# One layer of a hybrid conformer on one core: search vectors in PSUM, a second load buffer, eight gate matrices ahead of attention, and stores issued by ScalarE

## The chip, the cores and the metric

The kernel runs on one core of a Trainium2 chip. The metric is the device time of one execution in microseconds (us). Engines are called PE (TensorE, matmuls), PEld (its weight loads), DVE (VectorE), ACT (ScalarE), POOL (GpSimd) and SP (SyncE, which here only starts DMAs); SPq, DVEq and ACTq are their sequencers.

## The reference

One layer of a streaming encoder, in float32, on 1024 prompt frames and 64 sample frames (1088 together) of width 1024:

```python
h = x + 0.5 * _swiglu(x, ffn1_norm, ffn1_w_in, ffn1_w_out)
u = _rms(h, mix_norm)
z = u @ w_in                       # q | k | v | q_idx | k_idx | w_idx | conv_in | gate
...
score = jnp.einsum('bqh,bqhs->bqs', wi, jax.nn.relu(s))     # s: indexer queries x indexer keys
_, sel = lax.top_k(score, top)                              # top = min(256, L // 4)
...                                # softmax attention of each query over its selected keys
conv_out = jax.nn.silu(_layernorm(dc, conv_ln_g, conv_ln_b)) @ conv_w_out   # dc: depthwise conv, 31 taps
g_a, g_c = jnp.split(jax.nn.sigmoid(gate + b_gate), 2, axis=-1)
merged = g_a * (attn @ attn_w_out) + g_c * conv_out
h = h + merged @ w_out
h = h + 0.5 * _swiglu(h, ffn2_norm, ffn2_w_in, ffn2_w_out)
```

and a final norm. Outputs are the frames and the new keys, values, indexer keys and conv states.

## The kernel before

**Arithmetic.** Every float32 product is made of three matmuls: each operand is split into a high and a low part, and `mm3` adds hi x hi, hi x lo and lo x hi (L154, L155, L156). Weights come raw from HBM by SP (`raw`, L135), ACT rounds them to the high part (`whi`, L136), POOL subtracts to get the low part (`wlo`, L137). Activations are split the same way by `split`: the high part on ACT (L170), the low part on DVE or POOL (L171). A matmul of 128 x 128 weights moves one chunk of frames; there are three chunks, of 364, 362 and 362 frames.

**Stages.** The first feed-forward part; the projections, the conv (each tap a product `pd` on ACT, L694, and an addition on POOL, L695) and the indexer scores `Y` (L807 to L815), one row for each frame in seven tiles; then the search; then attention; then the second feed-forward part and the norm.

**The search** finds, for every frame, the threshold that leaves the wanted number of scores. It runs on DVE alone (L854 to L912). A first threshold comes from mean and spread of each row (L854 to L867). Six rounds follow, each with seven counts (L871, one per tile, result in `cnt`), and after each but the last some ten operations on 128x7 vectors (L876 to L888) that move the threshold `thr`. Then each tile gets the scores below the threshold (`F`, L897), their eight largest (L898), as many of them marked as the count is short (L899, L900), and a mask (`bias`, L904, with its count `seen`). Flags are formed and a branch (L914) is taken on DVE; its body is a slower search for rows whose count is off. The search has a high scheduling priority.

**K, V and the first queries.** `load_k` (L712 to L717), the load of V and `load_q` (L700 to L708) each bring raw data into a buffer `raw2` and split it. K, V and q share that buffer.

**Gates.** `gates` makes 16 matrices of gates, each in three chunks of 24 matmuls: 48 chunks. Each chunk's PSUM bank goes through a tanh on ACT (`sg`, L942), and SP stores it (L943). The first `GPRE` matrices are written ahead of attention, the others are background work inside it.

**Attention.** 36 units: nine tiles of queries by four pairs of heads. `soft` makes logits (`lg`, L989 and L990), adds the mask and takes the maximum on DVE (L992, `mb`), exponentials on ACT (L1002), scaling; `turn` transposes the weights into `pt` and splits them (`ph`, `pl`); `values` multiplies with V into `pv`, ACT copies that to `oh` (L1042), and SP stores it (L1043). Logits are made two units ahead. Between the steps `fill` takes `FILL[tile]` steps from a background generator: the rest of the gates, norm and output product of the conv (`gc`, L1122 to L1124), the merge of the third chunk (`ga`, L1147 to L1154), its product with `w_out` (`hr`, L1165, with loads at L1172 and stores at L1173) and the merge of the second chunk. Once attention is over, `h` is loaded again in three pieces (L1242) and the other products with `w_out` follow.

**Order.** A scheduler places the instructions of each engine by priorities and by its own model of time, so that the order on an engine isn't that of the code. Each engine works its list in order. SP's DMAs and, where it starts any, ACT's are counted on eight shared semaphores, and a DMA that takes one over waits for the one before it.

Of the kernel before, what the change touches and what calls it, by code (L numbers as in the profile page):

```python
# [95 lines left out]
def search_table():  # L96

    nd = NormalDist()
    t = np.zeros((P, 14, NT), np.float32)
    for n, (t0, rows, k0, L, top_) in enumerate(STILES):  # L100
        for half in range(2):
            r = slice(64 * half, 64 * half + 64)
            A = L - 64 * (1 - half) * (rows == P)
            z = nd.inv_cdf(1 - (top_ - 4) / A)
            t[r, 0, n], t[r, 1, n] = z, 1 / (A * nd.pdf(z))
        t[:, 2:6, n] = top_ - 3.9, top_, 1 / L, NEG * (L - top_)
    t[:, 6:] = np.tile(np.arange(8), NT).reshape(8, NT)
    return t.reshape(P, -1)


class Kern:
# [342 lines left out]
    def run(self):  # L454
        tc, nc, a = self.tc, self.nc, self.a
        PS = bass.MemoryType.PSUM
        with ExitStack() as top:
# [240 lines left out]
            def load_q(pool, src, t0, rows, qpool=None, qb=2, n=1280):  # L698

                raw = pool.tile([P, n], F32, name="raw2", tag="raw2")[:, 0:1024]  # L700
                raw = raw.rearrange("p (h c) -> p h c", h=8)[:, :, :rows]
                for i in range(4):
                    nc.sync.dma_start(raw[32 * i:32 * i + 32],
                                      src[i % 2, :, t0:t0 + rows].rearrange("(h r) c -> r h c", r=32))
                qt = (qpool or pool).tile([P, 8, P], F32R, name="qt", tag="qt", bufs=qb)[:, :, :rows]
                nc.scalar.activation(qt, raw, AF.Copy)
                nc.vector.tensor_tensor(qt[64:], raw[64:], qt[64:], op=ALU.subtract)
                return qt  # L708

            def load_k(pool, r0, name, tmp=None):  # L710
                kh = pool.tile([P, KCOLS], F32R, name=f"kh{name}")
                kl = pool.tile([P, KCOLS], F32R, name=f"kl{name}")  # L712
                raw = (tmp or pool).tile([P, 1280], F32, name="raw2", tag="raw2")[:, 0:KCOLS]
                for i in range(4):
# [46 lines left out]
            for i in (0, 1):  # L761
# [5 lines left out]
            small = lambda n, w=NT: kp.tile([P, w], F32, name=n)  # L767
            cnt, seen, exc, was, step, slope, gate, thr, unit = (
                small(n) for n in ("cnt", "seen", "exc", "was", "step", "slope", "gate", "thr", "unit"))
            sums = small("sums", 2 * NT)  # L770
            best = kp.tile([P, NT, 8], F32, name="best")
            rank = kp.tile([P, NT, 8], F32, name="rank")
            flags = kp.tile([P, 32], F32, name="flags")
# [22 lines left out]
            for n in SORD:  # L796
# [56 lines left out]
            v = nc.vector  # L853
            v.tensor_tensor(step, sums[:, 0:2 * NT:2], sums[:, 1:2 * NT:2], op=ALU.add)  # L854
# [4 lines left out]
            v.tensor_scalar(exc.bitcast(I32), slope.bitcast(I32), -0.5, 1597463007.0, op0=ALU.mult, op1=ALU.add)  # L859
            for i in range(2):  # L860
                v.tensor_tensor(gate, slope, exc, op=ALU.mult)
                v.scalar_tensor_tensor(gate, gate, -0.5, exc, op0=ALU.mult, op1=ALU.mult)
                v.scalar_tensor_tensor(exc, gate, 1.5, exc, op0=ALU.add, op1=ALU.mult)
            v.tensor_tensor(slope, slope, exc, op=ALU.mult)
            v.tensor_tensor(thr, slope, quant, op=ALU.mult)
            v.tensor_tensor(thr, thr, step, op=ALU.add)
            v.tensor_tensor(unit, slope, inv, op=ALU.mult)  # L867
            for r in range(ROUNDS):
                for n in range(NT):
                    rows, y0, L = rows_of(n)  # L870
                    v.tensor_scalar(spare(n), Y[:rows, y0:y0 + L], thr[:rows, n:n + 1], 0.0,  # L871
                                    op0=ALU.is_ge, op1=ALU.add, accum_out=cnt[:rows, n:n + 1])
                if r == ROUNDS - 1:
                    break
                exc, was = was, exc
                v.tensor_tensor(exc, cnt, goal, op=ALU.subtract)  # L876
                v.tensor_tensor(gate, exc, exc, op=ALU.mult)
                if r:
                    v.scalar_tensor_tensor(slope, was, 0.001, exc, op0=ALU.add, op1=ALU.subtract)
                    v.reciprocal(slope, slope)  # L880
# [3 lines left out]
                else:  # L884
                    v.tensor_copy(step, exc)
                v.scalar_tensor_tensor(gate, gate, 16.9, step, op0=ALU.is_gt, op1=ALU.mult)
                v.tensor_tensor(gate, gate, unit, op=ALU.mult)
                v.tensor_tensor(thr, thr, gate, op=ALU.add)  # L888

            v.tensor_tensor(gate, wanted, cnt, op=ALU.subtract)  # L890
            v.tensor_tensor(rank, gate.rearrange("p (n o) -> p n o", o=1).to_broadcast([P, NT, 8]),
                            zt[:, 6 * NT:].rearrange("p (n o) -> p n o", o=8), op=ALU.is_gt)
            v.tensor_scalar(rank, rank, 2 * STOP, -STOP, op0=ALU.mult, op1=ALU.add)
            for n in range(NT):
                rows, y0, L = rows_of(n)
                f = F[:rows, y0:y0 + L]
                v.scalar_tensor_tensor(f, spare(n), -STOP, Y[:rows, y0:y0 + L], op0=ALU.mult, op1=ALU.add)  # L897
                v.max(best[:rows, n, :], f)  # L898
                v.tensor_tensor(best[:rows, n, :], best[:rows, n, :], rank[:rows, n, :], op=ALU.min)  # L899
# [36 lines left out]
            def gates(ms, pool):  # L936
                for m, off in ms:
                    wt = self.wload(off, 1024)
                    for c, (c0, w) in enumerate(CHUNKS):
                        p = uproj(wt, c)  # L940
                        sg = pool.tile([P, WMAX], F32, name="sg", tag="sg", bufs=3)[:, :w]
                        nc.scalar.activation(sg, p, AF.Tanh, bias=hb[:, m:m + 1], scale=0.5)  # L942
                        nc.sync.dma_start(d_g[m, :, c0:c0 + w], sg)  # L943
                        yield
# [83 lines left out]
            def values(u, slot, ph, pl):  # L1028
# [9 lines left out]
                if last:  # L1038
                    if u.h0 == 6:
                        done.add(u.i)  # L1040
                    oh = ap_.tile([64, 256], F32, name="oh", tag="oh", bufs=2)[:, :n]
                    nc.scalar.activation(oh, u.pv, AF.Copy)  # L1042
                    nc.sync.dma_start(  # L1043
                        d_at[64 * u.h0:64 * u.h0 + 128, u.t0:u.t0 + u.rows].rearrange("(h d) c -> d h c", d=64),
# [196 lines left out]
            for c0, w in CHUNKS[::-1]:  # L1241
                nc.sync.dma_start(h[:, :, c0:c0 + w], d_h[:, :, c0:c0 + w])  # L1242
            tp = self.pool(top, "tp2", 6)
# [182 lines left out]
```

## Time and profile before

| | us |
|---|---|
| median of 3 runs (lowest, highest) | 2435.06 (2434.07, 2438.32) |
| the profiled execution | 2435.61 |
| its span | 2433.8 |
| PE busy | 2307.9 (95%) |
| DVE busy | 1677.8 (69%) |
| POOL busy | 1404.1 (58%) |
| ACT busy | 1146.8 (47%) |

The span is what the profile shows between the first and the last instruction; 1.8 us lie around it. The profiled execution is 0.55 us above the median. A row of the timeline or of the groups names the line, the engine, the operation, the tile written and the tiles read. A row of waits reads "engine tile line <- who released it: total us, times, longest".

### The profile page before, as it was taken

Reading aid. Unit: us, or ns where it says so; the run is one execution under the profiler, and the core shown is the slowest. Engines: PE = TensorE matmul, PEld = TensorE weight load, DVE = VectorE, ACT = ScalarE, POOL = GpSimd, SP = SyncE. Lnnn points to the kernel's source line nnn. Section 1 sums busy time; section 2 is a strip of 40 time slices with the busy share of each in tenths; the row PEclk is TensorE's granted clock in tenths of the full one; section 3 lists DMA queues with packets and bytes.
Section 4 is the critical chain, followed back from the end, with each engine's and each line's share of the span. In section 5 each row is a group of like instructions: output and inputs, shape, how many; then the busy total and the mean of one; then the engine's idle time right before and its main releaser. Section 6 shows DMA issues by size and latency. Waiting matters only on the chain.

```text
span 2433.8 us, 43946 instructions
## 1 busy us (share of the span) xinstructions
PE 2307.9 (95%) x16762; PEld 2278.1 (94%) x16762; DVE 1677.8 (69%) x3600; ACT 1146.8 (47%) x2189; POOL 1404.1 (58%) x861
## 2 busy tenths in 40 slices
PE   5999999999999999989699888799999999999998
PEld 5999999999999999989699888799999999999997
DVE  7666678666678386689634897358666677776676
ACT  5434445434346556865554664235443445433343
POOL 4555555555557786888662444457555555555554
PEclk9999999999999999999899999899999999999999
DMA  4222223223224344333223345752232322332223
GB/s 164 96 96 96 93 99 122 98 88 105 96 90 137 126 136 126 95 113 100 63 83 110 102 143 173 261 175 101 87 105 87 100 99 80 110 104 102 96 96 116
DMA packets 130118, 271.92 MB, mean 112 GB/s; under 512 B 18032, under 2 KB 77296, under 8 KB 129904
## 3 DMA queue, kind: packets, MB, share of 16 engines
q1 hardware_dynamic: 129904, 269.08, 33.1%
q8 instruction: 132, 2.16, 0.4%
q14 instruction: 82, 0.67, 0.1%
HBM read 230.34 MB, written 38.75 MB: 111 GB/s over the span
## 4 chain that ended last, share of the span: by engine, by line
PE 40%; DVE 6%; DMA 3%; issue 1%; ACT 1%; POOL 0%; SPq 0%; DVEq 0%; ACTq 0%
PE ps L154 12%; PE ps L156 12%; PE ps L155 12%; DMA ga<-d_g 1%; PE pt L1016 1%; DVE ga L1153 1%; DMA d_mp<-gc 1%; PE lg L989 1%; PE lg L990 0%; PE ps L184 0%; DVE pr L992 0%; PE pv L154 0%; DMA hr<-d_h 0%; DMA gc<-d_g 0%; PE pv L155 0%
## 5 line engine op out<-in xcount | busy, mean ns | idle before, releaser
L137 POOL TENSOR_TENSOR wlo<-raw,whi 128x1024 fp32r<-128x1024 f32 (+1 forms) x187 | 435.4, 2333 | 421.9 <-ACT whi L136 406.7
L154 PE MATMUL ps<-x,wp 128*128 128x272 f32 x1760 | 508.8, 291 | 11.2 <-DVE spare L302 9.2
L156 PE MATMUL ps<-x,wp 128*128 128x272 f32 x1760 | 506.3, 291 | 1.0 <-DVE wp L171 0.4
L155 PE MATMUL ps<-x,wp 128*128 128x272 f32 x1760 | 506.9, 289 | 0.0
L154 PE MATMUL ps<-x,whi 128*128 128x272 f32 (+2 forms) x1544 | 483.2, 313 | 18.2 <-ACT sg L942 8.8
L156 PE MATMUL ps<-x,wlo 128*128 128x272 f32 (+2 forms) x1544 | 481.5, 312 | 0.0
L155 PE MATMUL ps<-x,whi 128*128 128x272 f32 (+2 forms) x1334 | 412.3, 309 | 0.0
L154 PE MATMUL ps<-gh,whi 128*128 128x272 f32 x1408 | 400.0, 289 | 6.8 <-DVE spare L302 5.0
L155 PE MATMUL ps<-gl,whi 128*128 128x272 f32 x1408 | 404.9, 289 | 0.0
L156 PE MATMUL ps<-gh,wlo 128*128 128x272 f32 x1408 | 403.8, 288 | 0.0
L171 POOL TENSOR_TENSOR wlo<-raw,whi 128x1024 fp32r<-128x1024 f32 x88 | 220.1, 2502 | 263.8 <-ACT whi L170 260.6
L154 PEld LDWEIGHTS ps<-x,wp 128*128 128x128 f32 x1760 | 333.1, 189 | 12.2 <-ACT wp L170 12.2
L155 PEld LDWEIGHTS ps<-x,wp 128*128 128x128 f32 x1760 | 333.6, 190 | 0.0
L156 PEld LDWEIGHTS ps<-x,wp 128*128 128x128 f32 x1760 | 331.0, 189 | 2.3 <-DVE wp L171 1.7
L154 PEld LDWEIGHTS ps<-x,whi 128*128 128x128 f32 x1544 | 293.1, 190 | 20.3 <-ACT sg L942 9.3
L171 POOL TENSOR_TENSOR wp<-s,wp 128x512 fp32r<-128x512 f32 x176 | 258.7, 1470 | 90.0 <-ACT wp L170 90.0
L136 ACT ACTIVATE whi<-raw 128x1024 fp32r<-128x1024 f32 (+1 forms) x187 | 190.7, 1020 | 234.8 <-PE ps L155 127.2
L156 PEld LDWEIGHTS ps<-x,wlo 128*128 128x128 f32 x1544 | 292.9, 190 | 1.0
L442 DVE SCALAR_TENSOR_TENSOR h<-ps,h 128x272 f32<-128x272 f32 x384 | 164.7, 439 | 184.7 <-PE ps L156 184.2
L695 POOL TENSOR_TENSOR ac<-ac,pd 128x559 f32<-128x559 f32 x180 | 259.8, 1444 | 45.8 <-ACT pd L694 15.5
L154 PEld LDWEIGHTS ps<-gh,whi 128*128 128x128 f32 x1408 | 263.0, 189 | 8.3 <-DVE spare L302 5.7
L156 PEld LDWEIGHTS ps<-gh,wlo 128*128 128x128 f32 x1408 | 265.8, 189 | 0.0
(236 smaller groups left out, 4815.3 us busy)
## 6 DMA issues: line engine op xcount, KB each, us to landing
raw<-wf SPq DMA_DIRECT2D x334, 512.0 KB, 3.2
raw<-wf SPq DMA_DIRECT2D x32, 384.0 KB, 3.0
d_g<-sg SPq DMA_DIRECT2D x32, 181.0 KB, 1.9
d_h<-h SPq DMA_DIRECT2D x2, 2176.0 KB, 10.4
y<-t SPq DMA_DIRECT2D x32, 136.0 KB, 1.8
raw<-d_q SPq DMA_DIRECT2D x32, 128.0 KB, 2.7
raw<-d_qi SPq DMA_DIRECT2D x24, 128.0 KB, 3.0
d_g<-sg SPq DMA_DIRECT2D x16, 182.0 KB, 2.0
```

What stands on the lines that cost most here:

```text
L136: nc.scalar.activation(hi[:, :n], raw[:, :n], AF.Copy)
L137: self.weng.tensor_tensor(lo[:, :n], raw[:, :n], hi[:, :n], op=ALU.subtract)
L154: t.matmul(out, wh, xh, start=first, stop=False)
L155: t.matmul(out, wh, xl, start=False, stop=False)
L156: t.matmul(out, wl, xh, start=False, stop=last)
L171: (eng or nc.vector).tensor_tensor(lo, x, hi, op=ALU.subtract)
L442: nc.vector.scalar_tensor_tensor(x, p, 0.5, x, op0=ALU.mult, op1=ALU.add)
L695: nc.gpsimd.tensor_tensor(ac, ac, pd, op=ALU.add)
L989: nc.tensor.matmul(o, q, kh[:, ks:ks + pw], start=True, stop=False)
L1016: nc.tensor.transpose(pt[:kn, o:o + r], u.pr[hh][:, kk:kk + kn], ident[:r, :r])
L1153: nc.vector.scalar_tensor_tensor(ga, mpt, 0.5, ga, op0=ALU.mult, op1=ALU.add)
```

## The change

It has four parts.

1. `GPRE` goes from 2 to 8, so eight gate matrices (24 chunks) stand ahead of attention instead of two (6 chunks), and `FILL` for the sample tile from 4 to 2.
2. Search: the vectors `goal`, `over`, `slope`, `gate` and `cen` and the table `rank` lie in one PSUM bank, `srch`, instead of SBUF. Where two SBUF vectors were the operands of a 128x7 operation, one of them is now in PSUM; for that the excess is formed twice (`exc` in SBUF, `over` in PSUM), and the mean as well (`mean`, `cen`). Both inputs remain in SBUF for the first sum and for a few others, among them the mask. The rank test is against `goal` with a shifted table, which decides alike.
3. `raw2` has two buffers in attention's pools, and one in the indexer's.
4. ACT, not SP, starts the 48 gate stores, the 36 stores of attention outputs and the three reloads of `h`.

```diff
-GPRE = 2
+GPRE = 8
...
-FILL = {7: 1, 6: 1, 8: 4, 5: 1, 4: 1, 3: 2, 2: 2, 1: 2, 0: 2}
+FILL = {7: 1, 6: 1, 8: 2, 5: 1, 4: 1, 3: 2, 2: 2, 1: 2, 0: 2}
...
-    t[:, 6:] = np.tile(np.arange(8), NT).reshape(8, NT)
+    t[:, 6:] = np.tile(np.arange(8) - 3.4, NT).reshape(8, NT)
...
-                raw = pool.tile([P, n], F32, name="raw2", tag="raw2")[:, 0:1024]
+                raw = pool.tile([P, n], F32, name="raw2", tag="raw2", bufs=2 if n == 1280 else 1)[:, 0:1024]
...
-                raw = (tmp or pool).tile([P, 1280], F32, name="raw2", tag="raw2")[:, 0:KCOLS]
+                raw = (tmp or pool).tile([P, 1280], F32, name="raw2", tag="raw2", bufs=1 if tmp else 2)[:, 0:KCOLS]
...
-            quant, inv, goal, wanted, per, expect = (zt[:, i * NT:(i + 1) * NT] for i in range(6))
+            quant, inv, target, wanted, per, expect = (zt[:, i * NT:(i + 1) * NT] for i in range(6))
...
-                nc.scalar.activation(spare(n), y, AF.Square, accum_out=cnt[:rows, n:n + 1])
+                nc.scalar.activation(spare(n), y, AF.Square, scale=L ** -0.5, accum_out=cnt[:rows, n:n + 1])
...
-            v.tensor_tensor(step, sums[:, 0:2 * NT:2], sums[:, 1:2 * NT:2], op=ALU.add)
-            v.tensor_tensor(step, step, per, op=ALU.mult)
-            v.tensor_tensor(cnt, cnt, per, op=ALU.mult)
-            v.tensor_tensor(slope, step, step, op=ALU.mult)
+            bank = lgi.tile([P, 512], F32, name="srch", tag="lgi")
+            goal, over, slope, gate, cen = (bank[:, 16 * i:16 * i + NT] for i in range(5))
+            rank = bank[:, 128:128 + 8 * NT].rearrange("p (n o) -> p n o", o=8)
+            v.tensor_copy(goal, target)
+            v.tensor_tensor(gate, sums[:, 0:2 * NT:2], sums[:, 1:2 * NT:2], op=ALU.add)
+            v.tensor_tensor(cen, gate, per, op=ALU.mult)
+            v.tensor_tensor(mean, gate, per, op=ALU.mult)
+            v.tensor_tensor(slope, cen, mean, op=ALU.mult)
...
+                v.tensor_tensor(over, cnt, goal, op=ALU.subtract)
                 v.tensor_tensor(exc, cnt, goal, op=ALU.subtract)
-                v.tensor_tensor(gate, exc, exc, op=ALU.mult)
+                v.tensor_tensor(gate, exc, over, op=ALU.mult)
                 if r:
-                    v.scalar_tensor_tensor(slope, was, 0.001, exc, op0=ALU.add, op1=ALU.subtract)
+                    v.scalar_tensor_tensor(slope, was, 0.001, over, op0=ALU.add, op1=ALU.subtract)
                     v.reciprocal(slope, slope)
...
-                    v.tensor_copy(step, exc)
+                    v.tensor_scalar(step, over, 1.0, None, op0=ALU.mult)
...
-            v.tensor_tensor(gate, wanted, cnt, op=ALU.subtract)
+            for n in range(NT):
+                rows, y0, L = rows_of(n)
+                f = F[:rows, y0:y0 + L]
+                count(n, spare(n))
+                v.scalar_tensor_tensor(f, spare(n), -STOP, Y[:rows, y0:y0 + L], op0=ALU.mult, op1=ALU.add)
+                v.max(best[:rows, n, :], f)
+            v.tensor_tensor(gate, goal, cnt, op=ALU.subtract)
...
-            raw = ak.tile([P, 1280], F32, name="raw2", tag="raw2").rearrange("p (b d) -> p b d", d=P)
+            raw = ak.tile([P, 1280], F32, name="raw2", tag="raw2", bufs=2).rearrange("p (b d) -> p b d", d=P)
...
-                        nc.sync.dma_start(d_g[m, :, c0:c0 + w], sg)
+                        nc.scalar.dma_start(d_g[m, :, c0:c0 + w], sg)
...
-                    nc.sync.dma_start(
+                    nc.scalar.dma_start(
                         d_at[64 * u.h0:64 * u.h0 + 128, u.t0:u.t0 + u.rows].rearrange("(h d) c -> d h c", d=64),
...
-                nc.sync.dma_start(h[:, :, c0:c0 + w], d_h[:, :, c0:c0 + w])
+                nc.scalar.dma_start(h[:, :, c0:c0 + w], d_h[:, :, c0:c0 + w])
```

In the changed kernel the lines from the search on have numbers that are higher by three to ten: the gate store is L953, the attention store L1053, the logits L999 and L1000, the reload L1252, the branch L924.

The scheduler gives the engines new orders. Three places matter.

SP around the two K loads (`raw2<-d_k`), before:

```order
L135 DMA raw_14249<-wf 128x1024
L715 DMA raw2_13612<-d_k_60 32x1216 x4
L943 DMA d_g_64<-sg_13675 128x364
L943 DMA d_g_64<-sg_13703 128x362
L943 DMA d_g_64<-sg_13731 128x362
L715 DMA raw2_13621<-d_k_60 32x1216 x4
L135 DMA raw_14388<-wf 128x1024
```

and now:

```order
L135 DMA raw_14100<-wf 128x1024
L715 DMA raw2_13618<-d_k_60 32x1216 x4
L715 DMA raw2_13627<-d_k_60 32x1216 x4
L937 DMA raw2_13635<-d_v_61 128x1152
L938 DMA raw2_13635<-d_v_61 64x128
L703 DMA raw2_13642<-d_q_58 32x8x64 x3
L135 DMA raw_14190<-wf 128x1024
```

Three gate stores stood between the two K loads; now the second follows the first at once, and V and the first queries come right behind.

ACT at the same place, now (the K splits are `kh0` and `kh1`):

```order
L952 ACTIVATE sg_13709<-ps_13684,hb_81 128x362
L170 ACTIVATE kh0_13616<-raw2_13618 128x1216
L953 DMA d_g_64<-sg_13709 128x362
L694 ACTIVATE pd_12241<-ci_12162,par_77 128x559
L170 ACTIVATE kh1_13625<-raw2_13627 128x1216
L694 ACTIVATE pd_12244<-ci_12162,par_77 128x559
```

The gate store (L953) now stands in ACT's own list, one or two places behind the tanh that it stores.

PE at the first logits that need the search's end, before:

```order
L154 MATMUL ps_14484<-x_9442,whi_14479 128x364
L155 MATMUL ps_14484<-u_9450,whi_14479 128x364
L156 MATMUL ps_14484<-x_9442,wlo_14480 128x364
L989 MATMUL lg_13872<-kh0_13610,qt_13641 64x192 [waits DVE_49]
L990 MATMUL lg_13872<-kl0_13611,qt_13641 64x192
L989 MATMUL lg_13897<-kh1_13619,qt_13641 64x192 [waits DVE_49]
```

and now:

```order
L1000 MATMUL lg_14413<-kl0_13617,qt_13647 64x192
L154 MATMUL ps_14453<-x_9436,whi_14448 128x364 [waits DVE_49]
L155 MATMUL ps_14453<-x_9444,whi_14448 128x364
L156 MATMUL ps_14453<-x_9436,wlo_14449 128x364 [waits Pool_49]
...
L155 MATMUL ps_14481<-x_9445,whi_14448 128x362
L999 MATMUL lg_14418<-kh0_13616,qt_13647 64x192 [waits DVE_49]
L1000 MATMUL lg_14418<-kl0_13617,qt_13647 64x192
L999 MATMUL lg_14443<-kh1_13625,qt_13647 64x192 [waits DVE_49]
```

The fourth logits matmul of attention (`lg_13872`, now `lg_14418`) waits for DVE's first mask addition after the branch. Between the first gate matmul and it PE's list holds 529 gate matmuls before and 609 now, counted down the list; after the first 580 of these stands `ps_14453`, whose bank is that of the search's vectors, so that it waits for the search to end. Later in PE's list, the gates are through when 72 logits matmuls are (92 before), the merge of the third chunk begins after 182 of them (after all 208 before), and the merge of the second chunk stands among the last units of attention, where before it came after them.

More of the change, by code (lines that the diff above doesn't have):

```diff
@@ L767, in run @@
             small = lambda n, w=NT: kp.tile([P, w], F32, name=n)
-            cnt, seen, exc, was, step, slope, gate, thr, unit = (
-                small(n) for n in ("cnt", "seen", "exc", "was", "step", "slope", "gate", "thr", "unit"))
+            cnt, seen, exc, was, step, mean, thr, unit, root = (
+                small(n) for n in ("cnt", "seen", "exc", "was", "step", "mean", "thr", "unit", "root"))
             sums = small("sums", 2 * NT)
             best = kp.tile([P, NT, 8], F32, name="best")
-            rank = kp.tile([P, NT, 8], F32, name="rank")
             flags = kp.tile([P, 32], F32, name="flags")
@@ L858, in run @@
+            v.tensor_copy(goal, target)
[3 more added lines that the diff above has]
+            v.tensor_tensor(slope, cen, mean, op=ALU.mult)
             v.tensor_tensor(slope, cnt, slope, op=ALU.subtract)
-            v.tensor_scalar(exc.bitcast(I32), slope.bitcast(I32), -0.5, 1597463007.0, op0=ALU.mult, op1=ALU.add)
+            v.tensor_scalar(root.bitcast(I32), slope.bitcast(I32), -0.5, 1597463007.0, op0=ALU.mult, op1=ALU.add)
@@ L860, in run @@
             for i in range(2):
[L861 to L864, printed above, removed]
+                v.tensor_tensor(gate, slope, root, op=ALU.mult)
+                v.scalar_tensor_tensor(gate, gate, -0.5, root, op0=ALU.mult, op1=ALU.mult)
+                v.scalar_tensor_tensor(root, gate, 1.5, root, op0=ALU.add, op1=ALU.mult)
@@ L865, in run, with count @@
+            v.tensor_tensor(slope, slope, root, op=ALU.mult)
             v.tensor_tensor(thr, slope, quant, op=ALU.mult)
-            v.tensor_tensor(thr, thr, step, op=ALU.add)
+            v.tensor_tensor(thr, thr, cen, op=ALU.add)
             v.tensor_tensor(unit, slope, inv, op=ALU.mult)
-            for r in range(ROUNDS):
-                for n in range(NT):
[L870 to L874, printed above, removed]
+            def count(n, out):
+                rows, y0, L = rows_of(n)
+                v.tensor_scalar(out, Y[:rows, y0:y0 + L], thr[:rows, n:n + 1], 0.0,
+                                op0=ALU.is_ge, op1=ALU.add, accum_out=cnt[:rows, n:n + 1])
@@ L875, in run @@
+            for r in range(ROUNDS - 1):
+                for n in range(NT):
+                    count(n, spare(n))
                 exc, was = was, exc
+                v.tensor_tensor(over, cnt, goal, op=ALU.subtract)
                 v.tensor_tensor(exc, cnt, goal, op=ALU.subtract)
-                v.tensor_tensor(gate, exc, exc, op=ALU.mult)
+                v.tensor_tensor(gate, exc, over, op=ALU.mult)
                 if r:
-                    v.scalar_tensor_tensor(slope, was, 0.001, exc, op0=ALU.add, op1=ALU.subtract)
+                    v.scalar_tensor_tensor(slope, was, 0.001, over, op0=ALU.add, op1=ALU.subtract)
@@ L888, in run @@
                 v.tensor_tensor(thr, thr, gate, op=ALU.add)
-            v.tensor_tensor(gate, wanted, cnt, op=ALU.subtract)
+            for n in range(NT):
+                rows, y0, L = rows_of(n)
+                f = F[:rows, y0:y0 + L]
+                count(n, spare(n))
+                v.scalar_tensor_tensor(f, spare(n), -STOP, Y[:rows, y0:y0 + L], op0=ALU.mult, op1=ALU.add)
+                v.max(best[:rows, n, :], f)
+            v.tensor_tensor(gate, goal, cnt, op=ALU.subtract)
             v.tensor_tensor(rank, gate.rearrange("p (n o) -> p n o", o=1).to_broadcast([P, NT, 8]),
@@ L896, in run @@
                 f = F[:rows, y0:y0 + L]
-                v.scalar_tensor_tensor(f, spare(n), -STOP, Y[:rows, y0:y0 + L], op0=ALU.mult, op1=ALU.add)
-                v.max(best[:rows, n, :], f)
                 v.tensor_tensor(best[:rows, n, :], best[:rows, n, :], rank[:rows, n, :], op=ALU.min)
```

## The prediction

> **What bounds the kernel now.** I read the page's busy rows first, then the waits of the whole run, then the windows and the timeline around the longest of them.
>
> ```profile
> span 2433.8 us, 43946 instructions
> PE 2307.9 (95%) x16762; PEld 2278.1 (94%) x16762; DVE 1677.8 (69%) x3600; ACT 1146.8 (47%) x2189; POOL 1404.1 (58%) x861
> ```
>
> TensorE (PE) is busy for 2307.9 of 2433.8 us, and the change takes no matmul away. So it can only give back PE's idle time, about 126 us, or a stretch at a lower clock. The waits say where that idle time lies near the changed lines:
>
> ```profile
> PE lg L989 <- DVE mb L992: 24.3, 5, 20.4
> PE ps L154 <- ACT sg L942: 8.8, 1, 8.8
> PE ps L154 <- DVE ga L1152: 14.6, 6, 6.7
> PE ps L154 <- DVE hr L1165: 5.1, 1, 5.1
> ACT kh L170 <- DMA raw<-d_k: 7.2, 1, 7.2
> ```
>
> (Columns: total us, times, longest.) The first row is one wait of 20.4 us for the threshold search on VectorE (DVE), the second one wait of 8.8 us for a gate activation. On the timeline both have their place:
>
> ```profile
> 1087.58 0.67 PE L154 MATMUL ps<-x,whi 128*128 128x364 f32 x1 [8.83 <-ACT sg L942]
> 1088.05 0.51 PE L155 MATMUL ps<-x,whi 128*128 128x364 f32 x1
> 1091.08 0.51 PE L156 MATMUL ps<-x,wlo 128*128 128x364 f32 x1
> 1152.93 0.33 PE L155 MATMUL ps<-u,whi 128*128 128x364 f32 x1
> 1153.10 0.33 PE L156 MATMUL ps<-x,wlo 128*128 128x364 f32 x1
> 1173.81 0.42 PE L989 MATMUL lg<-kh,qt 128*64 128x192 f32 x1 [20.38 <-DVE mb L992]
> ```
>
> Gate matmuls start 0.167 us apart (1152.93, 1153.10). PE stops at about 1153.4 with its gate work in front of the logits used up, and goes on at 1173.81. The windows show what follows, in four stretches up to the second feed-forward part (columns: length, busy of PE, PEld, DVE, ACT, POOL, granted clock, DMA share, GB/s):
>
> ```profile
> 1173.80:1328.00 154.20, 153.51 (x991) 148.40 (x992) 70.19 (x176) 85.94 (x167) 90.25 (x50) 0.99 0.26 84
> 1328.00:1488.00 160.00, 144.39 (x987) 134.27 (x985) 138.24 (x364) 98.57 (x222) 75.22 (x45) 0.97 0.45 137
> 1488.00:1585.00 97.00, 76.58 (x410) 74.27 (x411) 44.24 (x67) 29.72 (x50) 41.45 (x20) 0.88 0.71 239
> 1585.00:1677.00 92.00, 86.68 (x530) 85.19 (x529) 64.26 (x134) 41.92 (x82) 58.70 (x35) 1.00 0.42 137
> ```
>
> PE is idle there for 0.7, 15.6, 20.4 and 5.3 us: 42 us that the change may shrink or grow.
>
> **The change, part by part.** *The search.* DVE runs it without a gap:
>
> ```profile
> 1057.27 0.89 DVE L854 TENSOR_TENSOR step<-sums 128x7 f32<-128x7 f32 x1
> 1061.24 1.25 DVE L861 TENSOR_TENSOR gate<-slope,exc 128x7 f32<-128x7 f32 x1
> 1064.01 0.17 DVE L861 TENSOR_TENSOR gate<-slope,exc 128x7 f32<-128x7 f32 x1
> 1127.84 2.32 DVE L888 TENSOR_TENSOR thr<-thr,gate 128x7 f32<-128x7 f32 x1
> 1166.24 0.19 DVE L912 TENSOR_REDUCE flag<-turned 128x1 int32<-128x32 f32 x1
> 1173.40 0.35 DVE L992 CUSTOM_DVE_ANT_0 pr<-lg,bias 64x192 f32<-64x192 f32 x1 [6.98 <-DVEq L914]
> ```
>
> From 1057.27 to 1166.43 it takes 109.2 us, and the branch at L914 another 7.0. One and the same instruction, L861, takes 1.25 us and then 0.17. Of the 128x7 rows 22 are long, the first and the last of them being 1057.27 and 1127.84; together they take 28.5 us. All but a copy have two inputs in SBUF, and all lie while POOL is adding. Two neighbouring rows of equal size show what one PSUM operand does to that:
>
> ```profile
> L327 DVE TENSOR_TENSOR s<-ps,raw 128x512 f32<-128x512 f32 x88 | 60.0, 682 | 0.0
> L332 DVE TENSOR_TENSOR s<-raw,s 128x512 f32<-128x512 f32 x88 | 101.6, 1155 | 0.0
> L207 DVE TENSOR_TENSOR rt<-rv,ps 128x3 f32<-128x3 f32 (+1 forms) x9 | 1.4, 154 | 0.2
> ```
>
> With `ps` in PSUM 682 ns, with both in SBUF 1155. L207 shows that a tiny operation with a PSUM input costs 154 ns, no more than the 0.17 of the SBUF ones. The change puts one operand of 21 of the 22 long operations into PSUM (the sum of `sums` stays): 27.6 - 21 x 0.17 = 24.1 us less. Bounds: 0, if the long rows have another cause, and 24.1. I take 24.1, since the pair L327 and L332 is the nearest row. About six operations are added: 6 x 0.2 = 1.2.
>
> The Trainium skill, "Perfetto Trace Analysis", section "Optimizing Scalar/DVE Operations", speaks against it: it gives DVE an access overhead of about 60 ns on SBUF and 125 ns on PSUM. By that some 70 small operations would lose 65 ns each, an estimate of 4.6 us, and the search would gain 18 instead of 23. The 154 ns of L207 does not bear it out, so I leave it out.
>
> A shorter search has a price of its own:
>
> ```profile
> L897 DVE SCALAR_TENSOR_TENSOR F<-bias,Y 128x384 f32<-128x384 bf16 (+6 forms) x7 | 13.1, 1929 | 0.0
> L904 DVE SCALAR_TENSOR_TENSOR bias<-F,fill 128x384 bf16<-128x384 f32 (+6 forms) x7 | 5.3, 801 | 0.0
> 1150.99 2.85 POOL L695 TENSOR_TENSOR ac<-ac,pd 128x559 f32<-128x559 f32 x2 [3.56 <-ACT ac L690]
> ```
>
> L904 (the mask) now runs from 1159 on, after POOL's last tap at 1153.8; L897, with the same shapes and POOL busy, takes 1929 ns. Begun 17 us earlier, the seven masks meet POOL: between 0 and 7 x 1.1 = 7.9 us; I take 7. The search ends at 1057.3 + 109.2 - 24.1 + 1.2 + 7 = 1150.6, the branch at 1157.6, and the first `mb` is there at 1158.0, instead of 1173.7.
>
> *The K loads.* What made PE wait 8.8 us is on SP's queue:
>
> ```profile
> 1060.78 9.01 SPq L943 DMA_DIRECT2D d_g<-sg  x3
> 1081.20 0.35 SPq L943 DMA_DIRECT2D d_g<-sg  x1
> 1477.32 0.58 SPq L1043 DMA_DIRECT2D d_at<-oh  x1
> 1524.72 0.58 SPq L1242 DMA_DIRECT2D h<-d_h  x1
> SPq L943 <- ACT sg L942: 106.8, 34, 6.7
> ```
>
> The three gate stores stand on SP between the first and the second K load and hold it until 1074.08; the second K split on ScalarE (ACT) then waits 7.2 us for that load, and the gate activation queued behind it frees no PSUM bank for PE. With a second `raw2` buffer and the stores on ACT, the two loads stand next to each other, so the 8.8 us go. Behind that wait 13 matmuls start some 0.30 us apart instead of 0.167 (the second and the last of them are at 1088.05 and 1091.08): about 1.8 us more. Together 10.6; below, if K still comes late, 0.
>
> *More gates ahead (GPRE, FILL).* In PE's order 609 gate matmuls, not 529, stand between the last indexer work and the fourth logits matmul, the one that waits for `mb`: 80 x 0.167 = 13.3 us of work pulled forward. The first 51 of them lead to a PSUM bank that the search holds to its end.
>
> *Sum at PE.* PE reaches that bank at 1153.4 - 10.6 + 51 x 0.167 = 1151.3, and the search ended at 1150.6: no wait. After 29 more matmuls, 1156.1, it waits until 1158.0: 1.9 us are left of 20.4. Gain: 8.8 + 1.8 + 20.4 - 1.9 = 29 us. Without a shorter search PE would stand at the bank from 1151.3 to 1167.4, and later for another 2.8: gain 12. So this term lies between 12 (or about 2, with K late too) and 31.
>
> *What follows.* Gates end earlier against attention, and the merges of the third and second chunk, which ran with attention over (idle 20.4 us), are now interleaved with its end: I take 8 of the 19.7 us of the `ga` and `hr` rows (14.6 + 5.1) as hidden, bounds 0 and 19.7. Against that: attention's DVE, at 138.2 of 160 us, gets part of the merges' work too, and I charge 3 (bounds 0 and 15.6, as much again as that window is idle now). The 48 gate stores, 36 attention stores and 3 reloads now cost ACT 48 x 0.35 + 36 x 0.58 + 3 x 0.58 = 39 us of issue. ACT's load is 98.6 of 160 in the densest window; 36 x 0.58 = 21 us more make it 120 of 160, so most lies beside other work. But many stores share a semaphore with a load of SP's and must wait for its landing, and behind a waiting store stand the next exponentials and splits: I charge 4, bounds 0 and 36. The reload of h, 4.35 MB at the end of merging, where DMA moves 239 GB/s already, gets 3, bounds 0 and 10 (its landing takes 7 to 10 us). Tail: -8 + 3 + 4 + 3 = +2.
>
> 2435.6 - 29 + 2 = 2408.6 for the profiled execution, which lies 0.55 above the median: **2408 us**.
>
> The Trainium skill, "DMA: Bandwidth & Descriptors", section "Issuing engines are not separate DMA queues", holds that issuing from several engines saves only the sequencer's time to start a transfer. By that rule moving the stores is worth nothing where SP is off the path, and the 10.6 us would rest on the second buffer alone. No row of this trace separates the two.
>
> **Rivals.** *The search does not get shorter* (PSUM operands don't help, or DVE waits instead for the K, V and q splits that now stand in its first two rounds). For it: the row below has two SBUF inputs as well and is never long, so I don't know the whole rule. Against it: L327 and L332. It gives 12 - 2 = 10 us: 2425.
>
> ```profile
> L886 DVE SCALAR_TENSOR_TENSOR gate<-gate,step 128x7 f32<-128x7 f32 x5 | 0.8, 167 | 0.2
> ```
>
> *The tail takes the idle time back.* Gates that are done cannot fill PE any more while softmax runs. For it: the first window after the search is full (153.5 of 154.2) just because gates fill it, and 13.3 us of them are gone from there. Against it: 112 background steps still meet 112 fill slots. It gives 2408 + 13 = 2421.
>
> *Slower: ACT's own stores stop ACT.* ACT works in order. Each of the 36 attention stores comes right behind its copy of `oh`, ahead of the next exponentials; if issue (0.58) and a wait of some 0.4 for a load's landing (whose median is 3.2 us for a weight) fall on the chain each time, that is 36 us: 2408 + 36 = 2444. It decides from 27 us, 0.75 per store. For it: SP waited 106.8 us in total in those places, so the stores do have something to wait for; these are waits for ACT itself, which fall away when ACT issues. Against it: ACT has 61 us free in that window.
>
> ```profile
> raw<-wf SPq DMA_DIRECT2D x334, 512.0 KB, 3.2
> h<-d_h SPq DMA_DIRECT2D x2, 1448.0 KB, 7.1
> ```
>
> **How the numbers follow.** My forecast, 2408 (its own range 2397 to 2418), has 0.62; the search not shorter, 2425, 0.12; the tail takes it back, 2421, 0.12; slower, 2444, 0.14. About 0.2%, 4.9 us, is what a measurement of this kernel can tell from no change. The first and third case are faster but for a small part; of the second a quarter, and of the fourth a third, fall within 0.2%: faster 0.82, same 0.08, slower 0.10. The range goes from 2390, where the merges' idle time and the masks' price both fall away, to 2435, which leaves out most of the last case.
>
> **What would show it.** Right: the 128x7 rows of the search at 0.15 to 0.25 us and the search near 93 us; no PE wait for `sg` near 1080; the wait for `mb` under 5 us; the four windows' PE idle together near 42. Wrong: long small rows in the search still there, PE waits with ACT as releaser after 1160, or ACT waiting on a DMA in front of its stores. A sum of idle time in the tail over 70 us would turn the sign.

## The result, and the profile after

| | before | after |
|---|---|---|
| median | 2435.23 us (2434.07 to 2438.32) | 2395.25 us (2394.14 to 2395.94) |
| ratio, 95% interval | | 0.9833 (0.9816 to 0.985) |
| span of the profiled execution | 2433.8 us | 2392.3 us |

The change makes the kernel 40 us faster, 1.5 times the 27 us that were forecast. The time lies inside the whole range of the prediction (2390 to 2435), but 2 us below 2397 to 2418, the range of its main case. The page of the changed kernel, its span and busy rows:

```profile
span 2392.3 us, 43870 instructions
PE 2300.3 (96%) x16762; PEld 2272.8 (95%) x16762; DVE 1658.8 (69%) x3606; ACT 1146.8 (48%) x2189; POOL 1407.1 (59%) x861
```

PE's 16762 matmuls are the same, but PE is busy for 7.6 us less, and idle for 33.9 us less. Windows tell where. Three of the kernel before (columns as in the prediction: length, PE, PEld, DVE, ACT, POOL, clock, DMA share, GB/s):

```profile
0.00:1055.00 1055.00, 1016.75 (x7468) 1008.74 (x7469) 722.42 (x1524) 520.80 (x982) 646.77 (x427) 0.99 0.32 108
1055.00:1700.00 645.00, 573.76 (x3626) 554.06 (x3626) 444.73 (x993) 323.62 (x626) 362.13 (x208) 0.95 0.42 133
1700.00:2433.80 733.80, 717.36 (x5672) 715.34 (x5670) 510.67 (x1086) 302.40 (x582) 395.22 (x227) 0.99 0.29 98
```

and of the changed kernel, whose last one is cut to the same length:

```profile
0.00:1055.00 1055.00, 1016.41 (x7467) 1008.14 (x7468) 725.91 (x1524) 520.27 (x982) 646.15 (x427) 0.99 0.33 108
1055.00:1658.50 603.50, 566.63 (x3630) 549.58 (x3629) 423.31 (x998) 324.74 (x626) 367.49 (x208) 0.97 0.45 142
1658.50:2392.30 733.80, 717.27 (x5670) 715.09 (x5668) 509.57 (x1085) 301.82 (x582) 393.48 (x227) 0.99 0.30 98
```

First and last part agree to 0.4 us, so all of the 41.5 us lie in the middle, 645.0 against 603.5. There PE's idle time falls from 71.2 to 36.9 and its busy time, for the same matmuls but for a few at the edges, from 573.8 to 566.6. The waits of PE after, in that part:

```profile
PE lg L999 <- ACT sg L952: 6.9, 1, 6.9
PE pv L154 <- ACT oh L1052: 6.7, 4, 3.5
PE lg L999 <- DVE mb L1002: 2.6, 4, 1.7
PE ps L154 <- DVE ga L1162: 7.8, 5, 3.8
PE ps L154 <- DVE hr L1175: 0.6, 1, 0.6
```

The waits of 8.8 and 20.4 us are gone; a new one of 6.9 us stands at the first logits. So the sum of the prediction can be redone with what was measured:

| us, change against before | forecast | measured |
|---|---|---|
| idle at K loads and search (29.2 before) | -27.3 | -22.3 |
| PE busy, less time at a low clock | -1.8 | -7.1 |
| idle in the rest up to the second feed-forward part (42 before) | +2 | -12.0 |
| sum | -27 | -41.5 |

The search is what the prediction said it would be. Two of DVE's groups before (busy us, mean ns):

```profile
L888 DVE TENSOR_TENSOR thr<-thr,gate 128x7 f32<-128x7 f32 x5 | 4.1, 815 | 0.2
L881 DVE TENSOR_TENSOR slope<-slope,step 128x7 f32<-128x7 f32 x4 | 3.8, 942 | 0.1
```

and its groups after:

```profile
L894 DVE TENSOR_TENSOR thr<-thr,srch 128x7 f32<-128x7 f32 x5 | 0.8, 163 | 0.2
L887 DVE TENSOR_TENSOR srch<-srch,step 128x7 f32<-128x7 f32 x4 | 0.7, 174 | 0.1
L914 DVE SCALAR_TENSOR_TENSOR bias<-F,fill 128x384 bf16<-128x384 f32 (+6 forms) x7 | 11.4, 1672 | 0.0
L919 DVE TENSOR_TENSOR srch<-seen,zt 128x7 f32<-128x7 f32 x1 | 1.2, 1234 | 0.0
```

and its timeline:

```profile
1057.50 0.90 DVE L857 TENSOR_TENSOR srch<-sums 128x7 f32<-128x7 f32 x1
1151.44 0.18 DVE L922 TENSOR_REDUCE flag<-turned 128x1 int32<-128x32 f32 x1
1159.75 0.35 DVE L1002 CUSTOM_DVE_ANT_0 pr<-lg,bias 64x192 f32<-64x192 f32 x1 [8.13 <-DMA d_g<-sg]
```

What was L888 (815 ns) is now 163 ns, what was L881 (942) is 174. The masks went from 801 to 1672 ns: they do meet POOL, and cost 6.1 us. From 1057.5 to 1151.6 the search takes 94.1 us.

### The profile page after: what moved, and what is told of

Its sections match the earlier page's. It is cut to its first block, busy times and chain, and to the rows that moved or that the text cites. A ratio compares the mean times of both kernels' runs of the same rounds, so it can differ in the third digit from the quotient of the medians.

```text
span 2392.3 us, 43870 instructions
## 1 busy us (share of the span) xinstructions
PE 2300.3 (96%) x16762; PEld 2272.8 (95%) x16762; DVE 1658.8 (69%) x3606; ACT 1146.8 (48%) x2189; POOL 1407.1 (59%) x861
## 4 chain that ended last, share of the span: by engine, by line
PE 76%; DVE 9%; DMA 6%; POOL 4%; issue 2%; ACT 2%; SPq 0%; ACTq 0%; DVEq 0%; POOLq 0%
PE ps L154 24%; PE ps L156 24%; PE ps L155 24%; POOL ac L695 3%; DMA ga<-d_g 1%; PE pt L1026 1%; PE lgi L806 1%; PE lgi L807 1%; DMA d_h<-hr 1%; DVE ga L1163 1%; DMA raw<-wf 1%; DMA raw<-d_k 1%; PE ps L184 1%; DMA d_mp<-gc 1%; DVE t L229 1%
## 5 line engine op out<-in xcount | busy, mean ns | idle before, releaser
L137 POOL TENSOR_TENSOR wlo<-raw,whi 128x1024 fp32r<-128x1024 f32 (+1 forms) x187 | 435.9, 2335 | 352.3 <-ACT whi L136 343.5
L154 PE MATMUL ps<-x,wp 128*128 128x272 f32 x1760 | 508.4, 290 | 10.9 <-DVE spare L302 9.3
L154 PE MATMUL ps<-x,whi 128*128 128x272 f32 (+2 forms) x1544 | 483.1, 313 | 9.3 <-ACT x L170 4.3
L154 PE MATMUL ps<-gh,whi 128*128 128x272 f32 x1408 | 399.8, 289 | 6.8 <-DVE spare L302 5.0
L154 PEld LDWEIGHTS ps<-x,wp 128*128 128x128 f32 x1760 | 332.9, 189 | 11.7 <-ACT wp L170 11.6
L154 PEld LDWEIGHTS ps<-x,whi 128*128 128x128 f32 x1544 | 293.2, 190 | 11.3 <-ACT x L170 4.7
L154 PEld LDWEIGHTS ps<-gh,whi 128*128 128x128 f32 x1408 | 262.9, 189 | 8.3 <-DVE spare L302 5.7
```

The lines of the kernel that those rows point to most:

```text
L137: self.weng.tensor_tensor(lo[:, :n], raw[:, :n], hi[:, :n], op=ALU.subtract)
L154: t.matmul(out, wh, xh, start=first, stop=False)
```

## The experiments

Each kernel is compared with runs of the kernel before made with it; their medians were 2433.95 (first four), 2436.17 (next four) and 2437.02 us (last four). Times of kernels of different groups are therefore compared by their ratio to the kernel before.

**Where the search's vectors lie.** `u2` is the change with them in SBUF.

```diff
-            bank = lgi.tile([P, 512], F32, name="srch", tag="lgi")
+            bank = kp.tile([P, 192], F32, name="srch")
```

> The change with its search vectors in SBUF again (same instructions, same order, only where the vectors lie). Theory (two SBUF inputs collide with POOL): the 128x7 rows are long again, the search grows by 24 us less the 7 that masks and flags now lose to POOL, and PE waits some 15 to 20 us for the first mb: 2409 to 2416. Rival (the shorter search is due to other things, such as the new order): 2395.

Measured: 2415.55 us (ratio 0.9925, 0.99 to 0.995), 22 us behind the change's 0.9833. Waits of this kernel:

```profile
PE lg L999 <- DVE mb L1002: 15.4, 1, 15.4
PE lg L999 <- ACT sg L952: 8.6, 1, 8.6
```

and groups on DVE:

```profile
L887 DVE TENSOR_TENSOR srch<-srch,step 128x7 f32<-128x7 f32 x4 | 5.2, 1308 | 0.1
L914 DVE SCALAR_TENSOR_TENSOR bias<-F,fill 128x384 bf16<-128x384 f32 (+6 forms) x7 | 5.3, 799 | 0.0
```

The same instruction goes from 174 to 1308 ns when its second operand is in SBUF. The masks are cheap again, since they come later; the search ends at 1171.8, 20 us later than in the change, and that is what PE waits for. The theory's number holds.

**Is it POOL?** `x1` is the kernel before without 29 of the conv's 30 taps: their additions on POOL are left out, and their products on ACT with them.

```diff
-                    for j in range(1, CW):
+                    for j in range(1, 2):
```

> The kernel before without 29 of the conv's 30 additions per piece on POOL (and their products on ACT), so the conv is left out of the result for the most part. Theory (the long 128x7 rows of the search are collisions with POOL's additions): of the 22 long rows no more than 5 are left, those that meet a weight split on POOL, and the search takes 85 to 92 us instead of 109. Rival (the rows are long for another reason, such as the distance between dependent operations): 22 long rows, 109 us less little.

Measured: the search runs from 1047.42 to 1138.6, 91 us instead of 109, and four long 128x7 rows are left of 22. (The time of this kernel, 2412.24 us in a single run, says nothing about the change, since work is missing.) DVE's rows, and POOL's beside them:

```profile
1049.42 2.38 DVE L859 TENSOR_SCALAR exc<-slope 128x7 int32<-128x7 int32 x1
1053.24 2.39 DVE L865 TENSOR_TENSOR thr<-slope,zt 128x7 f32<-128x7 f32 x1
1082.49 2.33 DVE L876 TENSOR_TENSOR was<-cnt,zt 128x7 f32<-128x7 f32 x1
1114.14 2.35 DVE L890 TENSOR_TENSOR gate<-zt,cnt 128x7 f32<-128x7 f32 x1
1049.37 2.41 POOL L137 TENSOR_TENSOR wlo<-raw,whi 128x1024 fp32r<-128x1024 f32 x1 [10.25 <-ACT whi L136]
1053.20 2.40 POOL L137 TENSOR_TENSOR wlo<-raw,whi 128x1024 fp32r<-128x1024 f32 x1 [1.43 <-ACT whi L136]
1081.24 3.56 POOL L137 TENSOR_TENSOR wlo<-raw,whi 128x1024 fp32r<-128x1024 f32 x1 [13.67 <-ACT whi L136]
1109.49 6.98 POOL L137 TENSOR_TENSOR wlo<-raw,whi 128x1024 fp32r<-128x1024 f32 x1 [10.08 <-ACT whi L136]
```

Two of the four lie exactly beside a weight split on POOL and last as long as it does (2.38 beside 2.41, 2.39 beside 2.40). The other two begin inside a longer split and end with it: 1084.82 and 1116.49, where POOL ends at 1084.80 and 1116.47. Together with `u2` this shows the theory: a long row is a small DVE operation that waits for POOL's instruction to end. L897 falls from 1929 to 797 ns in this kernel as well.

**Part 1 undone, and part 2 alone.** `u1` and `s2`.

```diff
-GPRE = 8
+GPRE = 2
...
-FILL = {7: 1, 6: 1, 8: 2, 5: 1, 4: 1, 3: 2, 2: 2, 1: 2, 0: 2}
+FILL = {7: 1, 6: 1, 8: 4, 5: 1, 4: 1, 3: 2, 2: 2, 1: 2, 0: 2}
```

This makes `u1` of the change. `s2` has parts 3 and 4 undone as well, with the edits shown for `u3` and `u4` below, so that of the change only part 2 is left.

> The change with part 1 undone (GPRE 2, FILL[8] 4). Theory (parts 1 and 2 need each other): with only two gate matrices ahead of attention, PE's list reaches the bank of the search's vectors after 138 gate matmuls instead of 570, at about 1055 + 138 x 0.167 = 1079, and stands there until the search ends near 1151: some 70 us of idle, 63 more than the 6.9 of the change, so about 2455. Rival (part 1 only pulls 80 matmuls forward): 13 us lost, 2408.

> The kernel before with part 2 alone (the search's vectors in PSUM). Theory (the bank of these vectors is one that attention needs, and with two gate matrices ahead PE reaches it after 138 gate matmuls, at about 1079): PE stands there until the search ends near 1145 to 1151, as with part 1 undone: 2465 to 2480. Rival (parts add up): a search 15 to 17 us shorter, 2418 to 2421.

Measured: 2476.47 us (ratio 1.018, 1.0151 to 1.0209) and 2479.72 us (1.0179, 1.0162 to 1.0196). Both are slower than the kernel before. PE's timeline of `u1`, then that of `s2`:

```profile
1083.90 0.42 PE L999 MATMUL lg<-kh,qt 128*64 128x192 f32 x1 [5.05 <-ACT sg L952]
1142.69 0.67 PE L154 MATMUL ps<-x,whi 128*128 128x364 f32 x1 [57.56 <-DVE flags L920]
```

```profile
1099.10 0.39 PE L999 MATMUL lg<-kh,qt 128*64 128x192 f32 x1 [20.93 <-issue]
1144.81 0.67 PE L154 MATMUL ps<-x,whi 128*128 128x364 f32 x1 [44.52 <-DVE flags L920]
```

With two gate matrices ahead, PE's list comes to the search's bank after 138 gate matmuls (and the first logits) and stands there: 57.6 us in `u1`, 44.5 in `s2`, where a stop of 20.9 us before it has no releaser in the profile. `s2` came out as its theory had it. `u1` is slower than the expected 2455 by 21 us: 65.1 us of idle up to this place (2.5, 5.0 and 57.6) were foreseen within 5 us, but its rest has 45.8 us of idle against 30.0 in the change (110.9 less 65.1, and 36.9 less 6.9), and its busy time is 7.9 us longer. Most of the idle surplus lies in the merges: PE waits there 14.2 us for `ga` and 9.0 for `hr`, against 7.8 and 0.6 in the change, much as in the kernel before. It goes with part 1, as the next run shows, and not with the bank.

**Part 1 alone.** `s1` is the kernel before with the two constants of part 1.

> The kernel before with part 1 alone (GPRE 8, FILL[8] 2). Its search stays in SBUF and long, and the gate stores still stand between the K loads. Theory (part 1 gives the gain in the tail, since gates that are done let the merges start during attention): the 8.8 us wait stays, PE reaches the logits with 590 instead of 519 gate matmuls done and waits some 9 us for mb instead of 20.4, and the tail's idle time falls from 42 to about 30, with less time at a low clock: 2407 to 2413. Rival (the tail's gain came from the other parts): 2421 to 2425.

Measured: 2418.24 us (ratio 0.9931, 0.9911 to 0.9951), some 17 us faster than before, between the ranges of the theory and of the rival, and in neither. The middle part of its span, cut where PE takes up the logits that wait, as in the kernel before (second row) and the change (third):

```profile
1178.80:1681.20 502.40, 470.36 (x3046) 452.32 (x3047) 330.41 (x775) 260.92 (x533) 272.76 (x153) 0.98 0.45 142
```

```profile
1173.80:1700.00 526.20, 484.17 (x3095) 465.12 (x3096) 335.29 (x777) 270.26 (x547) 281.34 (x158) 0.96 0.43 140
```

```profile
1157.50:1658.50 501.00, 471.02 (x3053) 454.29 (x3054) 331.12 (x779) 265.30 (x537) 277.04 (x154) 0.97 0.45 144
```

PE is idle there for 32.0 us in `s1`, 42.0 before, 30.0 in the change. So part 1 alone brings the gain of this stretch, the tail: 10 of 12 us of idle. What it does not bring is the search: PE's waits of `s1` before the logits are

```profile
PE lg L989 <- ACT sg L942: 31.2, 1, 31.2
ACT qt L706 <- DVEq L914: 23.1, 1, 23.1
```

31 us in one place, where I expected 8.8 and 9 in two. ACT stops at a query split (L706) that waits for the branch, with gate activations queued behind it, and PE's logits wait for these.

**Parts 3 and 4 undone, singly and together.** `u3` has one `raw2` buffer, `u4` has all stores and the reload on SP, `k12` both; `s4` is the kernel before with part 4 alone.

For `u3`, and likewise in the loads of K and q:

```diff
-            raw = ak.tile([P, 1280], F32, name="raw2", tag="raw2", bufs=2).rearrange("p (b d) -> p b d", d=P)
+            raw = ak.tile([P, 1280], F32, name="raw2", tag="raw2").rearrange("p (b d) -> p b d", d=P)
```

For `u4`, and likewise for the attention stores and the reload of `h`:

```diff
-                        nc.scalar.dma_start(d_g[m, :, c0:c0 + w], sg)
+                        nc.sync.dma_start(d_g[m, :, c0:c0 + w], sg)
```

> The change with a single raw2 buffer (part 3 undone). Theory (the gate stores between the K loads were the cause, not the buffer): the second K load still follows the first one on SP and waits only for the first split, ACT waits a few us, PE nothing or up to 3 us: 2395 to 2399. Rival (the buffer was the cause): PE waits the 8.8 us again, 2404 or more.

> The change with all stores and the reload on SP again (part 4 undone). The K loads still stand together, since the second buffer lets SP issue them ahead of the stores. Theory (stores on ACT are worth nothing here, the second buffer alone frees the K loads): 2393 to 2398. Rival (SP's waits for ACT's results delayed the loads of the merging stretch, and that is where the 12 us of idle time went that the forecast did not have): 2403 to 2408.

> The change with parts 3 and 4 undone (parts 1 and 2 only). Theory (either the second buffer or the stores on ACT frees the K loads; with neither the wait of about 9 us is back near 1080, but most of it is taken out of the 18.5 us that PE waits at the first logits with a single buffer): 2404 to 2411. Rival (the two waits add up): 2413 to 2418.

> The kernel before with part 4 alone (stores and reload on ACT). The two K loads stand next to each other. Theory (the 8.8 us are on PE's list, but the search sets when the logits can go on): the wait of 8.8 us is gone, PE arrives at the logits some 10 us earlier and waits some 30 us instead of 20.4: 2433 to 2438, no gain. Rival (the 8.8 us count by themselves): 2424 to 2428.

Measured: `u3` 2407.56 us (0.9899, 0.9871 to 0.9927), `u4` 2394.17 (0.9834, 0.9805 to 0.9862), `k12` 2406.72 (0.9868, 0.9851 to 0.9884), `s4` 2435.70 (0.9999, 0.9988 to 1.001).

No worth of part 4 can be seen: undone, the time stays (0.9834 against 0.9833, each known to 0.2 or 0.3%), done alone, it stays too (0.9999). The idle time of the tail says the same: 28.5 us in `u4` and 30.0 in the change, 42.2 in `s4` and 42.0 in the kernel before. So the rival that SP's waits had cost the tail falls.

Part 3 is worth something between 8 and 16 us (`k12` against `u4`, `u3` against the change, by their ratios; by the spans of the profiled executions 13.1 and 9.6), but not as either theory of `u3` had it. PE waits nowhere near 1080 in `u3`, nor in `k12`, whose time came out as expected but whose wait there did not come back. Waits of `u3`:

```profile
PE lg L999 <- ACT sg L952: 18.5, 1, 18.5
ACT qt L706 <- DVEq L924: 12.9, 1, 12.9
DVE qt L707 <- ACT qt L706: 7.6, 1, 7.6
```

The search is no longer than in the change: its flag is there at 1152.2 (1151.6 in the change). But the second query split (L706) waits on ACT for the branch, 12.9 us, and two gate activations stand behind it in ACT's list, so that PE waits 18.5 us at the first logits instead of 6.9. DVE's 7.6 us lie behind the flag as well, from 1152.2 to 1159.7, and end with the same split. In the change this split stands twelve places further back, behind the gate activations. So the second buffer is worth what it is by the order that the scheduler then gives ACT; that a single buffer must lead to the worse order is not shown.

`s4` has no gain, as expected, but for another reason than I gave. SP, ACT and PE in `s4`:

```profile
1057.40 16.57 SPq L715 DMA_DIRECT2D raw<-d_k  x8
1077.01 1.22 ACT L170 ACTIVATE kh<-raw 128x1216 fp32r<-128x1216 f32 x1 [7.63 <-DMA raw<-d_k]
1085.80 0.67 PE L154 MATMUL ps<-x,whi 128*128 128x364 f32 x1 [9.22 <-ACT sg L942]
```

The two K loads are neighbours now, no store stands between them, and still SP needs 16.57 us for the eight issues and the wait of about 9 us is there. What holds the second load is the buffer: it comes free when DVE has split the first K, and that split stands behind a whole round of counts. In the kernel before that split is this row, and the second K load begins at 1074.08, right at its end:

```profile
1071.94 2.12 DVE L171 TENSOR_TENSOR kl<-raw,kh 128x1216 fp32r<-128x1216 f32 x1
1074.08 2.10 SPq L715 DMA_DIRECT2D raw<-d_k  x4
```

Which of the two comes last can change: in `k12` that split ends at 1067.5, the three stores on SP end at 1069.3, and the second K load begins at 1069.5, so there the stores hold it, by 2 us.

**Less contention, more room, more gates.** `v1` puts the masks' fill value and the expected counts into PSUM:

```diff
+            low_, want = bank[:, 80:81], bank[:, 96:96 + NT]
+            v.tensor_copy(low_, fill)
+            v.tensor_copy(want, expect)
...
-                v.scalar_tensor_tensor(spare(n), f[:rows, y0:y0 + L], 10 * LOW, fill[:rows].to_broadcast([rows, L]),
+                v.scalar_tensor_tensor(spare(n), f[:rows, y0:y0 + L], 10 * LOW, low_[:rows].to_broadcast([rows, L]),
...
-            v.tensor_tensor(gate, seen, expect, op=ALU.not_equal)
+            v.tensor_tensor(gate, seen, want, op=ALU.not_equal)
```

`v1p3` adds a third buffer for tap products to that, and `g10` is the change with `GPRE` 10.

```diff
-                        pd = cvp_.tile([P, 559], F32, name="pd", tag="pd", bufs=2)
+                        pd = cvp_.tile([P, 559], F32, name="pd", tag="pd", bufs=3)
```

> The change with the mask's fill value and the expected counts in PSUM too, so that the seven masks (L914) have one SBUF input. Theory (the masks collide with POOL, which delays both DVE and, by POOL and the tap products, ACT's gate activations): masks 800 ns instead of 1672, the search 7 us shorter, the wait of 6.9 us at the first logits down to 2 to 5: 2388 to 2394. Rival (that wait is ACT and POOL working through the taps, whatever DVE does): 2395.

> The version with the masks' operands in PSUM, and three buffers for the tap products instead of two. Theory (the 4.9 us left at the first logits are gate activations on ACT queued behind tap products that wait for POOL to free a buffer): with one more buffer ACT runs ahead, the wait falls to 0 to 2 us: 2385 to 2388. Rival (POOL's own work, not ACT's place in the queue, sets it): 2390.

> The change with GPRE 10. PE's list now has 714 gate matmuls ahead of the first logits, 24 us of work more, which covers the search to its end and the branch too. Theory (the more gates ahead, the earlier the merges, as long as attention still has fill): the 6.9 us wait goes, the tail stays near 30 us of idle: 2385 to 2391. Rival (attention, which starts 17 us later, lacks fill and waits on DVE): the tail's idle grows by more than 7 us: 2395 to 2405.

Measured: `v1` 2390.32 us (ratio 0.9816, 0.9798 to 0.9833), `v1p3` 2388.25 us (0.9798, 0.9782 to 0.9814), `g10` 2403.71 us (0.9865, 0.9843 to 0.9888). Groups on DVE in `v1`, and a wait of its PE:

```profile
L917 DVE SCALAR_TENSOR_TENSOR bias<-F,srch 128x384 bf16<-128x384 f32 (+6 forms) x7 | 5.3, 798 | 0.0
```

```profile
PE lg L1002 <- ACT sg L955: 4.9, 1, 4.9
```

The masks are back at 798 ns, and DVE has its flag at 1143.8 instead of 1151.6. PE gets only 2.0 of these 7.8 us. `v1p3` has the same 4.9 us, so the theory that one more buffer frees ACT falls, though its time fell to the edge of the range that the theory gave (2388.25 against 2385 to 2388); the profiled spans of the two, 2388.2 and 2387.3, are 0.9 apart. What sets this wait is not settled. POOL is busy for 90.5 of 102.5 us from 1055 to 1157.5 in the change, which speaks for its own work. Both versions are faster than the kernel before. Against the change it is 0.17% and 0.35%: the intervals overlap for `v1`, which leaves it open, and barely miss each other for `v1p3`.

`g10` goes the rival's way in time, not quite in mechanism. The wait at the first logits does not go away (6.2 us, still for a gate activation; it has only moved, to 1181), and the rest has 35.0 us of idle, 5 more than the change. The larger part is PE's busy time, 575.4 against 566.6 for the same matmuls. DVE's first mask addition waits until the last gate store ahead of attention has landed:

```profile
DVE pr L1002 <- DMA d_g<-sg: 31.8, 1, 31.8
```

In the change that wait is 8.1 us, the branch included. So in `g10` attention begins 24 us later for gate work that would also have served as fill.

## Why the prediction was right, and where not

*The search, part by part: right.* 24.1 less for 21 operations, 7 more for the masks, 1.2 more for added operations gave 93.3; it took 94.1. On the timelines the small operations, the added ones included, take 21.8 us less (22.9 forecast), the stretch from the last count on 7.8 more, and the splits of K, V and queries among them 1.0 less. Of the 7.8 the masks cost 6.1, and one row that I had not on the list 1.1 (L919, two SBUF inputs). `u2` and `x1` show the cause. That all 22 long rows lie beside POOL's additions was read too narrowly: the one at 1127.84 ends with a weight split (POOL L137, from 1127.73, 2.40 us), like those left in `x1`. The value by the Trainium skill, "Perfetto Trace Analysis", section "Optimizing Scalar/DVE Operations", 125 ns on PSUM against 60 on SBUF, does not show: operations with an operand in PSUM take 163 and 174 ns here, and L886, with both in SBUF, took 167 in the kernel before.

*"So the 8.8 us go", for the gate stores on SP: right in size by luck, wrong in cause.* The row that I read, three stores of 9.01 us between the two loads, was true, but the stores weren't what held the load: it waited for the one buffer, and so for DVE (`s4`). PE met the wait at its 139th gate matmul, counted from 1055.3 (1055.3 + 139 x 0.167 = 1078.5), where the banks of the gates ahead of attention end and those of attention begin. Part 1 moves that place behind 570 gate matmuls by the same count, and so removes the 8.8 us with or without parts 3 and 4 (`s1`, `k12`).

*"No wait" at the bank, and 1.9 us left of 20.4: wrong by 5 us.* PE does get to that place in time, as worked out (it stops at 1150.6; I had 1151.3). But the first logits stand just ahead of the gate matmul that needs the search's bank, in a bank that needs ACT's last gate activation, and ACT is behind. I had looked at DVE for this place, and not at ACT.

*"What follows ... +2": the step that failed.* It was -12.0. Of the 19.7 us of the `ga` and `hr` rows I took 8 as hidden, and 11.3 went (14.6 and 5.1 before, 7.8 and 0.6 after). The three charges, 3 for a denser DVE, 4 for ACT's stores and 3 for the reload, did not come: all other idle time there changed by -0.7 together, not by +10. The window of merging after, against 76.58 of 97.00 before (the two do not hold quite the same matmuls), shows the first:

```profile
1445.00:1545.00 100.00, 88.31 (x534) 85.50 (x533) 62.87 (x125) 42.85 (x93) 51.36 (x29) 0.95 0.67 215
```

11.7 us of idle instead of 20.4. `s1` shows that this comes with part 1, and `u4` and `s4` that no cost of ACT's stores can be seen. ACT at least had its room in the very row that I quoted, 98.6 of 160. One sign of being wrong did appear, PE waits with ACT as releaser after 1160: those for `oh` grew from 1.0 to 6.7 us. But with the stores on SP they are 7.2 (`u4`), and with part 1 alone 8.1 (`s1`), so the stores do not make them. Why the denser DVE cost nothing was not tried.

*The clock: mis-sized, 1.8 against 7.1 us.* I counted the slow matmuls behind one wait only. In the same rows, merging before took 76.58 us for 410 matmuls, 187 ns each, at a granted clock of 0.88; after, 88.31 for 534, 165 ns each, at 0.95. The mix of matmuls is not quite the same in the two, but the difference shows in equal ones too: the 64 of L154 on `ch` with 362 columns went from a mean of 359 to 337 ns.

*The rivals.* That the search does not get shorter falls (`u2` is what it would look like). That the tail takes the idle back falls for `GPRE` 8, and is seen in part with 10. That ACT's stores stop ACT falls: `u4` gives the same time. Here the Trainium skill, "DMA: Bandwidth & Descriptors", section "Issuing engines are not separate DMA queues", is borne out: with 84 stores and three reloads moved to another engine, the time is 0.9833 of the kernel before, and 0.9834 without.

*Taken together*, in ratios to the kernel before: part 1 alone 0.9931, parts 1 and 2 0.9868, parts 1 to 3 0.9834, all four 0.9833; but part 2 alone 1.0179. The parts don't add: part 2 is a loss without part 1. Part 3 alone was not run.

## What to carry to other kernels

When a load waits, look for what frees its buffer before blaming what stands beside it in the queue. A vector put into a PSUM bank cost nothing by itself here, but look in PE's list for the next user of that bank, since with too little work ahead of it the whole gain turned into a stall of 45 to 58 us. And where waits go, count the time at a lower clock behind each of them, not only the waits.

## What the runs showed of the hardware

One of the four rows that stayed long in `x1` is a TENSOR_SCALAR with a single SBUF input: L859, 2.38 us beside a POOL instruction of 2.41, where it takes 0.17 otherwise. So a single input is no safeguard by itself; the Trainium skill, "SBUF — State Buffer", section "Who interferes with whom", counts tensor_scalar and copies among the operations that can take the port pair shared with GpSimd, if their operands meet certain conditions, and this row and the copy L885 agree:

```profile
L885 DVE COPY step<-was 128x7 f32<-128x7 f32 x1 | 1.4, 1368 | 0.0
L882 DVE TENSOR_SCALAR slope<-slope 128x7 f32<-128x7 f32 x4 | 0.7, 171 | 0.1
```

Both rows are of the kernel before. The second shows that it need not happen: in these four a TENSOR_SCALAR was never long. What all four long rows of `x1` share is that they end within 0.03 us of the end of POOL's instruction.
